# Contrast adjustment of 48 image planes: sums moved to ScalarE, a tile ahead of the stores

## The chip, the cores and the metric

One Trainium2 chip, one core. The time is device microseconds of one execution; the figure for the kernel before is the median of three runs. The profile is of one profiled execution, with times in microseconds from the start of its span.

## The reference

The input x has 16 x 3 planes of 512 x 512 float32 values in [0, 1); the factor is 1.5.

```python
mean = np.mean(x, axis=(2, 3), keepdims=True)
return np.clip(mean + factor * (x - mean), 0, 1).astype(np.float32)
```

Every output value is factor * x + (1 - factor) * mean, clipped to [0, 1], with the mean taken over its own plane. So each plane must be read whole and summed before any value of it can be written. In and out together are 100.66 MB.

## The kernel before

The data is cut into 12 tiles of 128 partitions by 8192 float32 (4.19 MB). A plane fills 32 partitions of a tile, so a tile holds four planes. A ring in SBUF, `ring`, has room for 6 tiles; tile t lies in buffer t % 6.

The program is written in the order in which each engine is to work (`manual_schedule`): the instructions of an engine stand in the order of the source, and the framework adds the semaphore waits that the accesses to the tiles need.

Loads are issued by SyncE (line 76, in `load`): tile 0 in two parts (columns 0 to 2047, then the rest), tile 1, tiles 2 and 3 in one transfer, tiles 4 and 5 in one transfer. Later, the load of tile t + 6 follows the work on tile t in the program; it waits for the store of tile t, which empties its buffer. Stores are issued from ScalarE's queue (line 101, in `store`).

The work on a tile is `compute(t)`. VectorE sums columns 0 to 4351 of each partition (line 81) into one column of `sums`; ScalarE, beside it, sums the remaining 3840 columns with an activation that copies to `junk` and accumulates (line 84). Two matmuls (lines 86 and 87) with the constant matrix `blockw`, which holds (1 - factor) / 262144 in four 32 x 32 blocks and zero elsewhere, add the two partial sums over the 32 partitions of a plane and give the shift of every partition in column t of the PSUM tile `bias`. VectorE then multiplies by the factor and adds the shift in place (line 91), and clips in place (line 94). Then the store is issued. Tile 0 is finished in two parts, of 2048 and 6144 columns, each with its own store.

```python
for t in range(n_tiles):
    compute(t)
    if t + BUFS < n_tiles:
        load(t + BUFS)
```

So before, ScalarE's queue holds: sum of tile t, store of tile t, sum of tile t + 1, store of tile t + 1. VectorE's holds: reduction of t, two passes over t, reduction of t + 1.

Of the kernel before, what the change touches and what calls it, by code (L numbers as in the profile page):

```python
# [1 line left out]

# [4 lines left out]


P = 128  # L10
ROW = 8192
BUFS = 6
SHORT = 2048
FIRST = (SHORT, ROW - SHORT)
SUM = 4352


@with_exitstack
def kernel(
    ctx: ExitStack,  # L20
    tc: tile.TileContext,
    x: bass.AP,
    factor: float,
    out: bass.AP,
):

    nc = tc.nc
    f32 = mybir.dt.float32  # L30
    Alu = mybir.AluOpType
    Act = mybir.ActivationFunctionType

    B, C, H, W = x.shape
    n_img, n_pix = B * C, H * W
    ppi = n_pix // ROW
    per_tile = P // ppi
    n_tiles = n_img // per_tile
    assert ppi * ROW == n_pix and per_tile * n_tiles == n_img

    factor = float(factor)
    wconst = (1.0 - factor) / float(n_pix)

    x_f = x.rearrange("b c h w -> (b c h w)")
    out_f = out.rearrange("b c h w -> (b c h w)")

    def dram(ap, t, c0=0, c1=ROW):
        return bass.AP(tensor=ap.tensor, offset=t * P * ROW + c0, ap=[[ROW, P], [1, c1 - c0]])

    consts = ctx.enter_context(tc.tile_pool(name="consts", bufs=1))  # L50
    xpool = ctx.enter_context(tc.tile_pool(name="xpool", bufs=1))
    small = ctx.enter_context(tc.tile_pool(name="small", bufs=1))
    psum = ctx.enter_context(tc.tile_pool(name="psum", bufs=1, space=bass.MemoryType.PSUM))


    sums = small.tile([P, 2 * n_tiles], f32, name="sums")
    junk = small.tile([P, ROW - SUM], f32, name="junk")
    bias = psum.tile([P, n_tiles], f32, name="bias")

    blockw = consts.tile([P, P], f32, name="blockw")  # L60
    nc.gpsimd.memset(blockw, 0.0)  # L61
    for a in range(0, P, ppi):
        nc.gpsimd.memset(blockw[a : a + ppi, a : a + ppi], wconst)  # L63


    ring = xpool.tile([P, BUFS, ROW], f32, name="ring")

    def load(t, c0=0, c1=ROW, n=1):

        b = t % BUFS  # L70
        src = bass.AP(
            tensor=x_f.tensor,
            offset=t * P * ROW + c0,
            ap=[[ROW, P], [P * ROW, n], [1, c1 - c0]],
        )
        nc.sync.dma_start(out=ring[:, b : b + n, c0:c1], in_=src)  # L76

    def compute(t):
        xt = ring[:, t % BUFS, :]
        own = sums[:, 2 * t : 2 * t + 2]  # L80
        nc.vector.tensor_reduce(  # L81
            out=own[:, 0:1], in_=xt[:, 0:SUM], axis=mybir.AxisListType.X, op=Alu.add
        )
        nc.scalar.activation(out=junk, in_=xt[:, SUM:ROW], func=Act.Copy, accum_out=own[:, 1:2])  # L84
        shift = bias[:, t : t + 1]
        nc.tensor.matmul(shift, blockw, own[:, 1:2], start=True, stop=False)  # L86
        nc.tensor.matmul(shift, blockw, own[:, 0:1], start=False, stop=True)  # L87
        c = 0
        for n in FIRST if t == 0 else [ROW]:
            part = xt[:, c : c + n]  # L90
            nc.vector.tensor_scalar(  # L91
                out=part, in0=part, scalar1=factor, scalar2=shift, op0=Alu.mult, op1=Alu.add
            )
            nc.vector.tensor_scalar(  # L94
                out=part, in0=part, scalar1=0.0, scalar2=1.0, op0=Alu.max, op1=Alu.min
            )
            store(t, c, c + n)
            c += n

    def store(t, c0, c1):  # L100
        nc.scalar.dma_start(out=dram(out_f, t, c0, c1), in_=ring[:, t % BUFS, c0:c1])

    with tc.manual_schedule():
        load(0, c1=SHORT)
        load(0, c0=SHORT)
        load(1)
        load(2, n=2)
        load(4, n=2)
        for t in range(n_tiles):
            compute(t)  # L110
            if t + BUFS < n_tiles:
                load(t + BUFS)


# [1 line left out]
_INS = ['x', 'factor']  # L116
_OUTS = [((16, 3, 512, 512), 'float32')]

_NUMBERS = {'factor': 1.5}


# [26 lines left out]
```

## Time and profile before

| | |
|---|---|
| time, median of 3 runs | 239.16 us (239.13 to 239.31) |
| span of the profiled execution | 237.3 us, so the median lies 1.9 us above it |
| instructions in the profile | 285 |
| TensorE (matmul) busy | 14.1 us (6%), 48 records |
| VectorE busy | 163.1 us (69%), 38 instructions |
| ScalarE busy | 43.2 us (18%), 25 instructions |
| moved | 50.33 MB read, 50.33 MB written, 424 GB/s over the span |
| first load issued | 0.74 us |
| last store issued | 218.17 us |

The profiled execution has no time of its own beside its span in the records; what lies around the span is taken as the difference to the median. In the profile, PE is TensorE, DVE is VectorE, ACT is ScalarE and SP is SyncE; a q behind the name means that the engine's queue issues a transfer. A float32 matmul shows as two records, so the 24 matmuls of the program are 48 records. A group's line gives the source line, engine, operation, output and inputs with their sizes, how many there are, the busy time and the mean length of one in ns, and then how long the engine sat idle just before them and what ended that. A table of stretches gives, for each stretch of the span, the busy time of each engine, TensorE's granted clock, the share of the DMA engines in use and GB/s.

### The profile page before, as it was taken

Reading aid. Unit: us, or ns where it says so; the run is one execution under the profiler, and the core shown is the slowest. Engines: PE = TensorE matmul, PEld = TensorE weight load, DVE = VectorE, ACT = ScalarE, POOL = GpSimd, SP = SyncE. Lnnn points to the kernel's source line nnn. Section 1 sums busy time; section 2 is a strip of 40 time slices with the busy share of each in tenths; the row PEclk is TensorE's granted clock in tenths of the full one; section 3 lists DMA queues with packets and bytes.
Section 4 is the critical chain, followed back from the end, with each engine's and each line's share of the span. In section 5 each row is a group of like instructions: output and inputs, shape, how many; then the busy total and the mean of one; then the engine's idle time right before and its main releaser. Section 6 shows DMA issues by size and latency. Waiting matters only on the chain.

```text
span 237.3 us, 285 instructions
## 1 busy us (share of the span) xinstructions
PE 14.1 (6%) x48; PEld 12.0 (5%) x48; DVE 163.1 (69%) x38; ACT 43.2 (18%) x25; POOL 0.9 (0%) x9
## 2 busy tenths in 40 slices
PE   0010010001010001010010100100100100010000
PEld 0010010001010001010010100100100100010000
DVE  0079989048989328999989898891892795687000
ACT  2050230041050023050320504101400500500000
POOL 1000000000000000000000000000000000000000
DMA  7999999999999999999999999999999999999996
GB/s 297 410 442 442 421 442 359 456 439 441 442 436 414 403 431 442 442 442 442 436 442 436 414 409 425 442 442 442 442 436 442 436 420 403 425 442 442 442 442 265
DMA packets 3712, 100.66 MB, mean 424 GB/s; under 512 B 384, under 2 KB 384, under 8 KB 384
## 3 DMA queue, kind: packets, MB, share of 16 engines
q1 hardware_dynamic: 1840, 50.33, 49.7%
q10 hardware_dynamic: 1872, 50.33, 49.2%
HBM read 50.33 MB, written 50.33 MB: 424 GB/s over the span
## 4 chain that ended last, share of the span: by engine, by line
DMA 57%; DVE 29%; another core or an unknown queue 3%; PE 1%; SPq 1%; issue 0%; DVEq 0%
DMA ring<-in_x_dram 41%; DMA out_dram<-ring 16%; DVE sums L81 10%; DVE ring L91 9%; DVE ring L94 9%; PE bias L87 1%; SPq L76 1%; DVEq L91 0%
## 5 line engine op out<-in xcount | busy, mean ns | idle before, releaser
L81 DVE TENSOR_REDUCE sums<-ring 128x1 f32<-128x4352 f32 x12 | 56.2, 4683 | 45.7 <-DMA ring<-in_x_dram 45.7
L84 ACT ACTIVATE junk<-ring 128x3840 f32<-128x3840 f32 x12 | 40.8, 3403 | 163.3 <-DMA ring<-in_x_dram 107.5
L91 DVE TENSOR_SCALAR ring<-ring,bias 128x8192 f32<-128x8192 f32 (+2 forms) x13 | 54.1, 4163 | 8.9 <-PE bias L87 7.4
L94 DVE TENSOR_SCALAR ring<-ring 128x8192 f32<-128x8192 f32 (+2 forms) x13 | 53.3, 4099 | 0.4
L86 PE MATMUL bias<-sums,blockw 128*128 128x1 f32 x24 | 7.0, 361 | 190.8 <-ACT junk L84 190.8
L86 PEld LDWEIGHTS bias<-sums,blockw 128*128 128x128 f32 x24 | 6.0, 312 | 191.7 <-ACT junk L84 175.2
L87 PE MATMUL bias<-sums,blockw 128*128 128x1 f32 x24 | 7.0, 363 | 4.3 <-DVE sums L81 3.9
L87 PEld LDWEIGHTS bias<-sums,blockw 128*128 128x128 f32 x24 | 6.0, 311 | 5.3 <-DVE sums L81 5.0
L84 ACT ACTIVATION_READ_ACCUMULATOR junk<-ring 128x1 f32 x12 | 2.2, 186 | 0.0
L84 ACT ACT_TABLE_LOAD x1 | 1.3, 1283 | 0.7 <-PEq L129 0.7
L63 POOL MEMSET blockw<- 32x32 f32 x4 | 0.5, 117 | 0.2
L61 POOL MEMSET blockw<- 128x128 f32 x1 | 0.2, 204 | 0.3 <-POOLq L129 0.3
L129 POOL MEMSET const-bfloat16-1.0<- 128x1 bf16 x1 | 0.1, 111 | 0.0
L129 POOL MEMSET const-uint8-127<- 128x1 uint8 x1 | 0.1, 111 | 0.0
L129 POOL MEMSET const-float32-1.0<- 128x1 f32 x1 | 0.1, 108 | 0.0
L129 POOL MEMSET const-float32-0.0<- 128x1 f32 x1 | 0.1, 103 | 0.2 <-issue 0.2
## 6 DMA issues: line engine op xcount, KB each, us to landing
out_dram<-ring ACTq DMA_DIRECT2D x11, 4096.0 KB, 35.8
ring<-in_x_dram SPq DMA_DIRECT2D x7, 4096.0 KB, 49.7
ring<-in_x_dram SPq DMA_DIRECT2D x2, 8192.0 KB, 66.7
ring<-in_x_dram SPq DMA_DIRECT2D x1, 3072.0 KB, 11.7
out_dram<-ring ACTq DMA_DIRECT2D x1, 3072.0 KB, 28.2
ring<-in_x_dram SPq DMA_DIRECT2D x1, 1024.0 KB, 4.8
out_dram<-ring ACTq DMA_DIRECT2D x1, 1024.0 KB, 17.5
```

The lines of the kernel that those rows point to most:

```text
L61: nc.gpsimd.memset(blockw, 0.0)
L63: nc.gpsimd.memset(blockw[a : a + ppi, a : a + ppi], wconst)
L76: nc.sync.dma_start(out=ring[:, b : b + n, c0:c1], in_=src)
L81: nc.vector.tensor_reduce(out=own[:, 0:1], in_=xt[:, 0:SUM], axis=mybir.AxisListType.X, op=Alu.add)
L84: nc.scalar.activation(out=junk, in_=xt[:, SUM:ROW], func=Act.Copy, accum_out=own[:, 1:2])
L86: nc.tensor.matmul(shift, blockw, own[:, 1:2], start=True, stop=False)
L87: nc.tensor.matmul(shift, blockw, own[:, 0:1], start=False, stop=True)
L91: nc.vector.tensor_scalar(out=part, in0=part, scalar1=factor, scalar2=shift, op0=Alu.mult, op1=Alu.add)
L94: nc.vector.tensor_scalar(out=part, in0=part, scalar1=0.0, scalar2=1.0, op0=Alu.max, op1=Alu.min)
L129: nc = _bacc.Bacc("TRN2", target_bir_lowering=False, num_devices=1)
```

## The change

`compute` is taken apart into `add`, `shift_by`, `clip` and `store`. Tile 0 keeps the shared sum: VectorE reduces columns 0 to 4351 and ScalarE the rest, and two matmuls make its shift. From tile 1 on, ScalarE sums the whole tile (8192 columns) with one activation, which now copies each value onto itself in the ring instead of into `junk`; VectorE does no reduction; and one matmul makes the shift. `junk` and `FIRST` are gone.

The order changes too. In the program, the sum and the matmul of tile t + 1 now stand ahead of the clip and the store of tile t. For tile 0, the first part (2048 columns) is clipped and stored first, then tile 1 is summed, then the second part of tile 0 is clipped and stored. ScalarE's queue thus holds: sum of t + 1, store of t, sum of t + 2, store of t + 1. The loads and their order are the same, as are the sizes of the transfers.

```diff
-    def compute(t):
-        xt = ring[:, t % BUFS, :]
-        own = sums[:, 2 * t : 2 * t + 2]
-        nc.vector.tensor_reduce(
-            out=own[:, 0:1], in_=xt[:, 0:SUM], axis=mybir.AxisListType.X, op=Alu.add
+    def clip(t, c0, c1):
+        part = ring[:, t % BUFS, c0:c1]
+        nc.vector.tensor_scalar(
+            out=part, in0=part, scalar1=factor, scalar2=bias[:, t : t + 1],
+            op0=Alu.mult, op1=Alu.add,
         )
-        nc.scalar.activation(out=junk, in_=xt[:, SUM:ROW], func=Act.Copy, accum_out=own[:, 1:2])
-        shift = bias[:, t : t + 1]
-        nc.tensor.matmul(shift, blockw, own[:, 1:2], start=True, stop=False)
-        nc.tensor.matmul(shift, blockw, own[:, 0:1], start=False, stop=True)
...
+        nc.vector.tensor_scalar(
+            out=part, in0=part, scalar1=0.0, scalar2=1.0, op0=Alu.max, op1=Alu.min
+        )
+
+    def add(t, c0=0):
+        part = ring[:, t % BUFS, c0:ROW]
+        own = sums[:, 2 * t : 2 * t + 1]
+        nc.scalar.activation(out=part, in_=part, func=Act.Copy, accum_out=own)
+        return own
+
+    def shift_by(t, *parts):
+        for k, part in enumerate(parts):
+            nc.tensor.matmul(
+                bias[:, t : t + 1], blockw, part, start=k == 0, stop=k == len(parts) - 1
             )
...
-        for t in range(n_tiles):
-            compute(t)
+
+        rest = sums[:, 1:2]
+        nc.vector.tensor_reduce(
+            out=rest, in_=ring[:, 0, 0:SUM], axis=mybir.AxisListType.X, op=Alu.add
+        )
+        shift_by(0, add(0, SUM), rest)
+        clip(0, 0, SHORT)
+        store(0, 0, SHORT)
+        shift_by(1, add(1))
+        clip(0, SHORT, ROW)
+        store(0, SHORT, ROW)
+        load(BUFS)
+        for t in range(1, n_tiles):
+            if t + 1 < n_tiles:
+                shift_by(t + 1, add(t + 1))
+            clip(t, 0, ROW)
+            store(t, 0, ROW)
             if t + BUFS < n_tiles:
                 load(t + BUFS)
```

More of the change, by code (lines that the diff above doesn't have):

```diff
@@ L13 @@
 SHORT = 2048
-FIRST = (SHORT, ROW - SHORT)
 SUM = 4352
@@ L56 @@
     sums = small.tile([P, 2 * n_tiles], f32, name="sums")
-    junk = small.tile([P, ROW - SUM], f32, name="junk")
     bias = psum.tile([P, n_tiles], f32, name="bias")
@@ L76, in load @@
         nc.sync.dma_start(out=ring[:, b : b + n, c0:c1], in_=src)
-    def compute(t):
-        xt = ring[:, t % BUFS, :]
-        own = sums[:, 2 * t : 2 * t + 2]
-        nc.vector.tensor_reduce(
-            out=own[:, 0:1], in_=xt[:, 0:SUM], axis=mybir.AxisListType.X, op=Alu.add
-        )
-        nc.scalar.activation(out=junk, in_=xt[:, SUM:ROW], func=Act.Copy, accum_out=own[:, 1:2])
-        shift = bias[:, t : t + 1]
[L86 to L92, printed above, removed]
-            )
[L94 to L98, printed above, removed]
+    def clip(t, c0, c1):
[3 more added lines that the diff above has]
+            op0=Alu.mult, op1=Alu.add,
+        )
+        nc.vector.tensor_scalar(
[10 more added lines that the diff above has]
+                bias[:, t : t + 1], blockw, part, start=k == 0, stop=k == len(parts) - 1
+            )
     def store(t, c0, c1):
```

## The prediction

> **What bounds the kernel now.** I read the slices of the page first, then the table of stretches, then the groups of instructions, then the timeline around one tile and around the last one.
>
> ```profile
> DVE  0079989048989328999989898891892795687000
> ACT  2050230041050023050320504101400500500000
> DMA  7999999999999999999999999999999999999996
> ```
>
> ```profile
> 38.50:50.70 12.20, 0.00 (x0) 0.00 (x0) 3.43 (x2) 0.00 (x0) 0.00 (x0) 1.00 0.96 408
> 50.70:145.70 95.00, 7.04 (x24) 6.01 (x24) 81.27 (x19) 20.98 (x12) 0.00 (x0) 1.00 1.00 433
> 145.70:203.70 58.00, 3.52 (x12) 3.00 (x12) 40.78 (x9) 10.49 (x6) 0.00 (x0) 1.00 1.00 434
> 203.70:218.20 14.50, 1.18 (x4) 1.01 (x4) 13.60 (x3) 3.50 (x2) 0.00 (x0) 1.00 1.01 434
> ```
>
> The last two columns of a stretch are the share of the 16 DMA engines in use and GB/s. The DMA engines never rest: share 1.00 at 433 GB/s from 50.7 us to the end, at least 0.96 from 6 us on. The 100.66 MB of the page take 232.5 us at 433 GB/s, of a span of 237.3 us. So the kernel is bound by the transfers, and VectorE's 163 us lie beside them. Two things follow. No edit to the engines can gain much: what is left is some 4.8 us of start and finish, which the change does not touch. And the change is free only as long as the engines still bring the stores early enough to leave no DMA engine idle. How much room there is, the end of the timeline shows.
>
> ```profile
> 203.76 4.69 DVE L81 TENSOR_REDUCE sums<-ring 128x1 f32<-128x4352 f32 x1 [4.98 <-DMA ring<-in_x_dram]
> 213.71 4.43 DVE L94 TENSOR_SCALAR ring<-ring 128x8192 f32<-128x8192 f32 x1
> 218.17 0.34 ACTq L101 DMA_DIRECT2D out_dram<-ring  x1
> ```
>
> The last store is issued at 218.2 us and the span ends 19.1 us later; one tile of 4.19 MB alone is 9.7 us at 433 GB/s. So a whole store is still ahead of it in the queue. Counting two stores (19.4 us) and about 0.9 us for landing back from 237.3, store 9 leaves the DMA engines at about 217: store 10, issued at 198.8, is 18 us early, store 11 some 8 us.
>
> **The costs of a tile.** The groups, each shape apart, and one tile's timeline give every duration.
>
> ```profile
> L91 DVE TENSOR_SCALAR ring<-ring,bias 128x8192 f32<-128x8192 f32 x11 | 49.4, 4491 | 8.2 <-PE bias L87 6.7 <-issue 1.5
> L94 DVE TENSOR_SCALAR ring<-ring 128x8192 f32<-128x8192 f32 x11 | 48.7, 4427 | 0.4
> L84 ACT ACTIVATE junk<-ring 128x3840 f32<-128x3840 f32 x12 | 40.8, 3403 | 163.3 <-DMA ring<-in_x_dram 107.5 <-DVE ring L94 55.8
> L84 ACT ACTIVATION_READ_ACCUMULATOR junk<-ring 128x1 f32 x12 | 2.2, 186 | 0.0
> ```
>
> ```profile
> 50.73 3.40 ACT L84 ACTIVATE junk<-ring 128x3840 f32<-128x3840 f32 x1 [19.16 <-DMA ring<-in_x_dram]
> 54.28 0.58 PE L86 MATMUL bias<-sums,blockw 128*128 128x1 f32 x2 [21.44 <-ACT junk L84]
> 55.42 0.59 PE L87 MATMUL bias<-sums,blockw 128*128 128x1 f32 x2 [0.55 <-DVE sums L81]
> 56.11 4.49 DVE L91 TENSOR_SCALAR ring<-ring,bias 128x8192 f32<-128x8192 f32 x1 [0.75 <-PE bias L87]
> 60.64 4.43 DVE L94 TENSOR_SCALAR ring<-ring 128x8192 f32<-128x8192 f32 x1
> 65.10 0.34 ACTq L101 DMA_DIRECT2D out_dram<-ring  x1
> 65.48 3.40 ACT L84 ACTIVATE junk<-ring 128x3840 f32<-128x3840 f32 x1 [11.25 <-DVE ring L94]
> ```
>
> Read off: matmul 0.15 us after the sum's 3.40 us have passed (50.73 to 54.28); clip 0.69 us after the matmul starts (55.42 to 56.11); store issued 8.99 us after the clip starts (56.11 to 65.10); ScalarE's next instruction 0.38 us after that.
>
> **Removed.** Eleven VectorE reductions of 4.68 us (51.5 us) and eleven of the twenty-four matmuls. VectorE is not the bound, so this alone is worth nothing; it only shortens a tile's way from landing to store.
>
> **Added: the longer sum.** ScalarE sums 8192 elements where it summed 3840. No row has that length. If the whole 3403 ns scales, it is 7.26 us; if twice the accumulator's 186 ns is fixed, (3403-372) x 2.133 + 372 = 6.84 us. I take one such fixed part, (3403-186) x 2.133 + 186 = 7.05 us, the nearest to what ScalarE itself shows as a price without elements. Writing in place into the ring instead of into junk I cost at nothing: the same 128 partitions of f32 are written per element; 0.1 us either way would be inside these ends. The Trainium skill ("ScalarE: Activation LUTs", What ACT_TABLE_LOAD costs) gives 186 ns + 0.833 ns per element, 3.39 us for the row's 3.40, hence 7.01 us; the sum below would be 0.4 us less by it. The same page (Rules for kernel authors) speaks against the change: plain adds belong on VectorE.
>
> **Moved: the order, and two new waits.** This decides. On ScalarE the order is now add(t+1), store(t), add(t+2). ScalarE works its queue in order, so add(t+2), though its tile may have landed long ago, stands behind store(t), which waits for clip(t) on VectorE. That is the first wait. The second is not in the source: the built program's waits show that the first clip instruction of tile t waits for the matmul of tile t+1, not only for its own; the plainest sign is that the clip of the last tile waits for no TensorE semaphore at all, because the one before it has already waited for that matmul. All shifts are columns of the one tile `bias`, and the matmul of t+1 stands ahead of clip(t) in the program. So clip(t) stands behind add(t+1), and store(t) behind clip(t), and add(t+2) behind store(t): a closed ring through three engines with no overlap at all between ScalarE's sum and VectorE's clip. "A tile ahead" buys nothing; one turn is
>
> 7.05 (add) + 0.15 + 0.69 (matmul) + 8.99 (clip) + 0.38 (issue) = 17.26 us per tile.
>
> The DMA engines need 19.4 us per tile (8.39 MB in and out at 433 GB/s). So each turn is faster than the transfers, and once data is there the ring does not wait for loads. But it starts late and cannot catch up fast enough: before, tile 0 and 1 were stored while the first six loads still ran; now each store needs the next tile's landing.
>
> **When it starts.** Tile 0's loads, sum and first store (issued at 20.9) are unchanged. Tile 1 has landed about 9.6 us after tile 0 (12.9), at 22.5; add(1) runs from there, and the rest of tile 0's clip waits for its matmul: 22.5 + 7.05 + 0.84 = 30.4, its two clip instructions take 6.8 us (20.79 to 27.63 before), so store 0's second part is issued at 37.2 instead of 27.6. Add(2) needs tiles 2 and 3, which one load brings; before, they landed at 50.7. The stretch 38.5 to 50.7 moved 4.98 MB, shared by this load and store 0's second part; by their rows (32 and 24 KB, taken in turns, an estimate) 57% or 2.84 MB were the load's. Store 0's first part took 17.5 us to land (page, DMA issues) for an exchange that is 12.1 us by this sharing (5.24 MB at 433 GB/s), so a store joining busy queues starts some 4 us late: at 41.2. Until then the load has the DMA to itself (2.7 us, 1.17 MB), the other 1.67 MB at 57% take 6.9 us: add(2) starts at 48.2. The ends are 50.7 (no relief) and 45.1 (all 2.84 MB alone).
>
> **The sum.** Add(11) starts nine turns later: 48.2 + 9 x 17.26 = 203.5. Clip(10) starts at 203.5 + 7.05 + 0.84 = 211.4, store 10 is issued at 220.4, clip(11) follows at once and store 11 goes at 229.4, against 198.8 and 218.2 before. The DMA engines are done with everything else at about 217 (above), so they stand idle for 3 to 5 us until store 10 gets going, which was 18 us early before. Two stores from an idle start: the first as tile 0's load did, 12.1 us from issue to use (0.74 to 12.88), the second 9.7 us more: 220.4 + 21.8 = 242.2, and some 0.4 us to the end of the span: 242.6. Around the span lie 1.9 us (239.16, the median, less 237.3): 244.5 us, 2.2% slower. Loads do not bind: store 5, which frees the buffer of tile 11, is issued at about 134 and tile 11 is needed at 203.5, 69 us for a store and a load that take 39 us at half the rate each. Smaller edits (one matmul each, junk gone, SP's order) cost nothing beside this; SP's loads wait on later stores, but SP has nothing else queued.
>
> **Rivals.**
> A, no slower. The transfers stay the bound: the stores, though late, keep the queue filled to the end, and the time is 239.2 plus or minus 0.5. It decides where store 10 is issued before about 216, 4.6 us earlier than I have it: with ten sums of 6.6 us, with add(2) at 43.6, or if clip(t) did not truly wait for the next tile's matmul, which would let VectorE clip under the next load. For: 17.26 is below 19.4. Against: 6.6 is below my low end of 6.84, and the waits stand in the program. Chance 0.09; 0.08 same, with a 0.01 tail to faster.
> B, worse still: the sum is 7.26 us (2.1 us more over ten sums) and the first stores bring no relief to load 2 (2.5 us): 246.6 to 249, chance 0.12. The stretch 38.5 to 50.7 speaks for it, with only 408 GB/s where the stores had just begun.
> C, the change gains: the stretches below 433 GB/s between 20.9 and 50.7 (420 and 408) come from mixing stores in, and fewer stores there save up to 0.9 us without a later idle time: 238.3. Needs A first; chance 0.02.
>
> **How the numbers follow.** My case has 0.77, at 244.5. Its ends: 6.84 us gives -2.1, 7.26 gives +2.1, add(2) between 45.1 and 50.7 gives -3.1 to +2.5, the four small gaps of a turn at 0.05 us each 0.5 to 1 us; not all on one side. The range 241.0 to 247.5 takes these, and leaves out A, C and the far part of B. A measurement of this kernel can tell about 0.2% (0.5 us). Faster 0.03, same 0.08, slower 0.89.
>
> **What would show it.** After: ScalarE's ACTIVATE on 128x8192 near 7.05 us; VectorE's clip idle before it "<-PE bias" some 8 us at each of ten tiles, adding to over 80 us; starts of successive sums 17.3 us apart from about 48 us on, with tiles landed long before; the last store issued near 229; a slice with DMA below 9 around 217 to 222. Wrong if the clip of tile t runs while the sum of t+1 does, if sums are spaced by 19.4 us waiting for loads, or if the DMA slices stay full to the end.

## The result and the profile after

The changed kernel takes 242.85 us (median of four runs, 242.81 to 244.06) against 239.14 us before: ratio 1.0163, 95% interval [1.0146, 1.018], slower by 1.6%. The profiled execution took 242.83 us with a span of 241.0 us.

The slices of the page after, VectorE, ScalarE and the DMA engines:

```profile
DVE  0074091007709509429239159068076095099800
ACT  2052900091290380560650830920902903800000
DMA  7999999989999999999999999999999999986996
```

VectorE has lost its reductions but that of tile 0 and is busy for 112 us instead of 163, with holes wherever ScalarE is busy: the two take turns. What ends the kernel is in the third row. The DMA slices, full to the end before, open in the last fifth. The table of stretches (us; busy time and count by engine; TensorE's clock, DMA share, GB/s in the last columns) sizes the hole:

```profile
145.70:203.70 58.00, 1.76 (x6) 1.50 (x6) 31.53 (x8) 22.47 (x7) 0.00 (x0) 1.00 1.00 434
203.70:220.00 16.30, 0.59 (x2) 0.50 (x2) 9.57 (x3) 6.02 (x2) 0.00 (x0) 1.00 0.75 322
```

A quarter of 16.3 us is 4.1 us of idle DMA engines; the span is 3.7 us longer. The groups of instructions and the list of waits give the cause:

```profile
L89 ACT ACTIVATE ring<-ring 128x8192 f32<-128x8192 f32 x11 | 77.3, 7029 | 115.1 <-DVE ring L82 90.7 <-DMA ring<-in_x_dram 24.4
L78 DVE TENSOR_SCALAR ring<-ring,bias 128x8192 f32<-128x8192 f32 x11 | 49.4, 4491 | 92.8 <-PE bias L94 92.8
```

```profile
DVE ring L78 <- PE bias L94: 103.0, 12, 18.5
ACT ring L89 <- DVE ring L82: 90.7, 9, 10.1
```

VectorE's clip waits for a matmul at every tile but the last, and ScalarE's sum waits for VectorE's clip (through the store that stands ahead of it) at nine tiles: 10.1 us each time, the length of a clip with its handovers. ScalarE's three waits for loads all end by 48 us. One turn and the end, from the timeline:

```profile
47.78 7.03 ACT L89 ACTIVATE ring<-ring 128x8192 f32<-128x8192 f32 x1 [18.21 <-DMA ring<-in_x_dram]
...
64.95 7.03 ACT L89 ACTIVATE ring<-ring 128x8192 f32<-128x8192 f32 x1 [10.04 <-DVE ring L82]
...
72.12 0.58 PE L94 MATMUL bias<-sums,blockw 128*128 128x1 f32 x2 [16.58 <-ACT ring L89]
72.75 4.49 DVE L78 TENSOR_SCALAR ring<-ring,bias 128x8192 f32<-128x8192 f32 x1 [8.21 <-PE bias L94]
77.27 4.43 DVE L82 TENSOR_SCALAR ring<-ring 128x8192 f32<-128x8192 f32 x1
81.73 0.34 ACTq L99 DMA_DIRECT2D out_dram<-ring  x1
82.11 7.03 ACT L89 ACTIVATE ring<-ring 128x8192 f32<-128x8192 f32 x1 [10.04 <-DVE ring L82]
...
202.60 7.03 ACT L89 ACTIVATE ring<-ring 128x8192 f32<-128x8192 f32 x1 [10.10 <-DVE ring L82]
...
219.38 9.20 ACTq L99 DMA_DIRECT2D out_dram<-ring  x2
```

Sum, matmul, clip, store issue, next sum: no two overlap. At 72.75 VectorE starts on tile 2, and the matmul it waited for, at 72.12, is that of tile 3. Nine turns lead from 47.78 to 202.60, 17.20 us each. The stores of tiles 10 and 11 (merged in the last line) go at 219.4 and 228.2; before, 198.8 and 218.2. In shorter stretches no DMA packet starts between 215.5 and 220.2 us: the queue is dry, that is, nothing issued is left to move, until store 10 gets going.

### The profile page after: what moved, and what is told of

Same layout as the page of the kernel before. It is cut to its first block, busy times and chain, and to the rows that moved or that the text cites. A ratio compares the mean times of both kernels' runs of the same rounds, so it can differ in the third digit from the quotient of the medians.

```text
span 241.0 us, 218 instructions
## 1 busy us (share of the span) xinstructions
PE 7.6 (3%) x26; PEld 6.5 (3%) x26; DVE 112.0 (46%) x27; ACT 83.1 (34%) x25; POOL 0.9 (0%) x9
## 3 DMA queue, kind: packets, MB, share of 16 engines
q1 hardware_dynamic: 1840, 50.33, 48.9%
## 4 chain that ended last, share of the span: by engine, by line
DVE 39%; ACT 27%; DMA 19%; issue 5%; PE 2%; ACTq 1%; SPq 1%
ACT ring L89 27%; DVE ring L78 21%; DMA ring<-in_x_dram 19%; DVE ring L82 18%; PE bias L94 2%; ACTq L99 1%; SPq L74 1%; ACTq L89 0%
## 5 line engine op out<-in xcount | busy, mean ns | idle before, releaser
L89 ACT ACTIVATE ring<-ring 128x8192 f32<-128x8192 f32 (+1 forms) x12 | 80.7, 6727 | 125.9 <-DVE ring L82 90.7
L94 PE MATMUL bias<-sums,blockw 128*128 128x1 f32 x26 | 7.6, 361 | 202.8 <-ACT ring L89 202.1
L94 PEld LDWEIGHTS bias<-sums,blockw 128*128 128x128 f32 x26 | 6.5, 311 | 203.8 <-ACT ring L89 186.7
L109 DVE TENSOR_REDUCE sums<-ring 128x1 f32<-128x4352 f32 x1 | 4.7, 4686 | 12.8 <-DMA ring<-in_x_dram 12.8
L89 ACT ACTIVATION_READ_ACCUMULATOR ring<-ring 128x1 f32 x12 | 2.2, 186 | 0.0
## 6 DMA issues: line engine op xcount, KB each, us to landing
out_dram<-ring ACTq DMA_DIRECT2D x1, 1024.0 KB, 17.5
```

Source lines behind the costliest of these rows:

```text
L89: nc.scalar.activation(out=part, in_=part, func=Act.Copy, accum_out=own)
L94: nc.tensor.matmul(bias[:, t : t + 1], blockw, part, start=k == 0, stop=k == len(parts) - 1)
L109: nc.vector.tensor_reduce(out=rest, in_=ring[:, 0, 0:SUM], axis=mybir.AxisListType.X, op=Alu.add)
```

## The experiments

The theory has three parts: the closed ring (the clip of t waits for the matmul of t + 1; the sum of t + 2 stands behind the store of t), its length, and its late start. Twelve kernels ran, in three groups; the kernel before ran beside each group, at 239.23, 239.32 and 239.25 us.

| | time, us | ratio to before, 95% interval | store 10 issued, us |
|---|---|---|---|
| changed kernel | 242.85 | 1.0163 [1.0146, 1.018] | 219.4 |
| two bias tiles | 239.10 | 0.9992 [0.9983, 1.0002] | 204.0 |
| clip ahead of matmul | 239.04 | 0.9991 [0.9982, 1.0] | 203.7 |
| whole sum, own turn | 239.14 | 0.9994 [0.9984, 1.0003] | 207.4 |
| shared sum, ahead | 239.17 | 0.9998 [0.9989, 1.0008] | 207.0 |
| longer sum | 253.08 | 1.0586 [1.056, 1.0611] | 228.9 |
| sum of 7936 | 242.35 | 1.0121 [1.01, 1.0141] | 219.1 |
| sum of 7424 | 238.87 | 0.9982 [0.9973, 0.9992] | 214.4 |
| tiles 2, 3 apart | 244.63 | 1.0224 [1.0209, 1.0239] | 221.2 |
| tiles 2 to 5 apart | 241.67 | 1.0114 [1.009, 1.0137] | 219.6 |
| last turn opened | 238.95 | 0.9988 [0.998, 0.9997] | 212.1 |
| before, tile 0 whole | 240.01 | 1.003 [1.0017, 1.0042] | |
| clip first, tile 0 whole | 239.76 | 1.0014 [1.0005, 1.0023] | |

The time is a median; the issue of store 10 is read from the one profiled run of each kernel. In the five kernels that the closed ring made slower, the time of the profiled run lies 23.4 to 23.6 us after that issue (242.83 less 219.38 in the changed kernel, 252.37 less 228.93 with the longer sum, 244.74 less 221.19 with tiles 2 and 3 apart), whatever made store 10 late.

**Two bias tiles.** The first two kernels of the list after the changed one open the ring in two ways; the third takes the next tile's sum out from ahead of the store, and the fourth shortens the turn.

```diff
-    bias = psum.tile([P, n_tiles], f32, name="bias")
+    biases = [psum.tile([P, 512], f32, name=f"bias{k}") for k in range(2)]
+
+    def bias_of(t):
+        return biases[t % 2][:, t : t + 1]
...
-            out=part, in0=part, scalar1=factor, scalar2=bias[:, t : t + 1],
+            out=part, in0=part, scalar1=factor, scalar2=bias_of(t),
...
-                bias[:, t : t + 1], blockw, part, start=k == 0, stop=k == len(parts) - 1
+                bias_of(t), blockw, part, start=k == 0, stop=k == len(parts) - 1
```

> The changed kernel with the shifts of even and odd tiles in two PSUM tiles, so that the clip of a tile waits for its own matmul alone. Theory (the closed ring of sum, clip and store, which starts late, makes store 10 late): the clip of t runs while tile t + 1 is still loading, the ring is open, store 10 is issued before 216 and the time is back at 239.2 (238.7 to 239.7); VectorE's idle time before the clip for the matmul falls from 103 us by more than half. Rival (stores are late because ScalarE's queue holds store t behind the sum of t + 1, or because the whole sum stands on ScalarE): both are unchanged here, so 242 to 243.

239.10 us, as the theory has it, with ScalarE's order and its whole sums unchanged, which ends the rival. The waits of this kernel, of the two that answer to those shown above:

```profile
ACT ring L92 <- DMA ring<-in_x_dram: 127.4, 10, 22.8
DVE ring L81 <- PE bias L97: 95.7, 10, 19.4
```

ScalarE now waits for loads at ten tiles, no longer for VectorE: the transfers pace it. One part of my expectation was wrong: VectorE's idle time ahead of the clip stays at 95.7 us, and it did not fall by half, because it is now the wait for the tile's own landing and sum. The size of a wait does not tell whether it is in a ring; who ended the wait before it does.

**Clip ahead of the matmul.**

```diff
-        shift_by(1, add(1))
+        own = add(1)
         clip(0, SHORT, ROW)
+        shift_by(1, own)
...
-                shift_by(t + 1, add(t + 1))
+                own = add(t + 1)
             clip(t, 0, ROW)
+            if t + 1 < n_tiles:
+                shift_by(t + 1, own)
```

> The changed kernel with the matmul of tile t + 1 placed behind the clip of tile t in the program, the order on ScalarE and VectorE as in the changed kernel and one PSUM tile for the shifts. Theory: the clip no longer waits for the next tile's matmul, which opens the ring as two PSUM tiles do: 239.2 (238.7 to 239.7). Rival (the PSUM tile itself, or ScalarE's order, makes the loss): 242 to 243. If two PSUM tiles help and this does not, it is the place of the shifts and not the wait.

239.04 us with one PSUM tile. It is the wait and not the place of the shifts.

**Whole sum, own turn.**

```diff
-        shift_by(1, add(1))
...
-            if t + 1 < n_tiles:
-                shift_by(t + 1, add(t + 1))
+            shift_by(t, add(t))
             clip(t, 0, ROW)
             store(t, 0, ROW)
```

> The whole sum on ScalarE in place and one matmul, but in the order of the kernel before: sum, clip and store of a tile in its own turn. Theory: the turn is still 17.2 us without overlap, but a store no longer waits for the landing of the next tile, and 17.2 is less than the 19.4 us of the transfers: store 11 about 2.4 us later than before (220.6), no idle DMA, 239.2 (238.7 to 239.7). Rival (the turn of 17.2 us is itself the loss, whatever the order): 241 or more.

239.14 us. From this kernel's timeline:

```profile
190.56 7.03 ACT L89 ACTIVATE ring<-ring 128x8192 f32<-128x8192 f32 x1 [10.10 <-DVE ring L82]
207.35 0.34 ACTq L99 DMA_DIRECT2D out_dram<-ring  x1
207.79 7.03 ACT L89 ACTIVATE ring<-ring 128x8192 f32<-128x8192 f32 x1 [10.10 <-DVE ring L82]
224.57 0.34 ACTq L99 DMA_DIRECT2D out_dram<-ring  x1
```

The turn is the same 17.2 us, with the same waits of ScalarE for VectorE; but a sum is followed by the store of its own tile, so store 10 goes at 207.4 instead of 219.4. Store 11 is later than I expected (224.6 against 220.6), later too than before (218.2), and the time is the same: it still finds store 10 under way. So neither the whole sums nor the turn make the loss by themselves; store 10 beyond the point where the queue runs dry does.

**Shared sum, ahead.**

```diff
+    def shared(t):
+        rest = sums[:, 2 * t + 1 : 2 * t + 2]
+        nc.vector.tensor_reduce(
+            out=rest, in_=ring[:, t % BUFS, 0:SUM], axis=mybir.AxisListType.X, op=Alu.add
+        )
+        return add(t, SUM), rest
...
-        shift_by(1, add(1))
+        shift_by(1, *shared(1))
...
-                shift_by(t + 1, add(t + 1))
+                shift_by(t + 1, *shared(t + 1))
```

> The new order alone: the sum of t + 1 ahead of the clip of t, but shared between VectorE (4352) and ScalarE (3840) with two matmuls, as before. The clip still waits for the next tile's matmuls. Theory: the ring turns in 4.7 + 0.7 + 9.0 = 14.4 us, 2.8 us less than with the whole sum on ScalarE, so after ten turns store 10 is some 28 us earlier or waits for loads: 239.2 (238.7 to 239.9). Rival (waiting for the next tile is the loss by itself, whatever the length of the sum): 241 or more.

239.17 us. The order alone, with the ring closed, costs nothing while the turn is short (the store issues at 63.90 and 78.20 in its timeline are 14.3 us apart). The change needs both its parts to lose.

**A longer and two shorter sums.**

```diff
+MORE = 1024
...
+        if t:
+            nc.scalar.activation(out=junk, in_=part[:, 0:MORE], func=Act.Copy)
         nc.scalar.activation(out=part, in_=part, func=Act.Copy, accum_out=own)
```

The two shorter sums differ in one constant, 7936 or 7424:

```diff
+FEWER = 7936
...
-        part = ring[:, t % BUFS, c0:ROW]
+        part = ring[:, t % BUFS, c0 : ROW if t == 0 else FEWER]
```

> The changed kernel with a second activation of 1024 elements per tile on ScalarE ahead of each whole sum (its copy is not used). Theory: ten sums lie one behind the other in the ring between the landing of tiles 2 and 3 and the issue of store 10; the rows of 3840 and 8192 elements give 0.833 ns per element, so each turn grows by about 1.0 us and the time by ten times that: 252.8 (252 to 254), and the start of the second sum moves by 1 us at most. Rival (a fixed price, such as waiting for the first landings, with the sums beside the transfers): under 245.

> The changed kernel with ScalarE summing 7936 of the 8192 columns from tile 1 on (256 columns are left out of the mean). Theory: 0.21 us less in each of ten turns, 2.1 us less in all, still above the floor of the transfers: 240.7 (240.3 to 241.2). Rival (the loss is not proportional to the length of the sum): 242 to 243.

> The changed kernel with ScalarE summing 7424 of the 8192 columns from tile 1 on (768 columns are left out of the mean). Theory: ten turns of 0.64 us less would give 236.4, which is below the floor of the transfers; store 10 is issued near 213, before the queue runs dry, so 239.2 (238.8 to 239.7), no lower. Rival (no floor, the chain alone makes the time): 236 to 237.

253.08 us for the longer sum, against 252.8 expected: 1.06 us for each of the 1024-element activations, and 10.2 us in all between the medians. The four runs are two near 252.4 and two near 253.7; in the profiled one (252.37) store 10 goes 9.55 us later than in the changed kernel, ten activations less a second sum that starts 1.05 us earlier, at 46.73. The sum of 7424 meets the floor at 238.87 us, not the 236.4 us of a chain without one; store 10 goes at 214.4. The sum of 7936 is a miss: 242.35 us (241.39 to 242.53) for 240.7, within the band of the rival (242 to 243), by which the loss does not follow the length of the sum. The time alone would speak for the rival, so the timeline has to decide. ScalarE's:

```profile
49.07 6.82 ACT L90 ACTIVATE ring<-ring 128x7936 f32<-128x7936 f32 x1 [19.72 <-DMA ring<-in_x_dram]
...
202.46 6.82 ACT L90 ACTIVATE ring<-ring 128x7936 f32<-128x7936 f32 x1 [10.16 <-DVE ring L83]
...
219.09 9.20 ACTq L100 DMA_DIRECT2D out_dram<-ring  x2
```

Its turn is 153.39 / 9 = 17.04 us, shorter by 0.16 us of the 0.21 that the sum lost; but the ring started at 49.07 instead of 47.78, 1.3 us later. From the start to store 10 it is 170.02 us against 171.60: the gain per turn is there, and the later landing of tiles 2 and 3 took most of it away in this run of 242.53 us. That the run of 241.39 us had the earlier start is likely and not shown. Only the length per turn is shown here; the time of 240.7 was not reached.

**The start of the ring.**

```diff
-        load(2, n=2)
+        load(2)
+        load(3)
         load(4, n=2)
```

> The changed kernel with tiles 2 and 3 loaded by two transfers instead of one; the ring is untouched. Theory: tile 2 lands about 10 us earlier, the ring starts near 38 instead of 47.8, and store 10 is issued before 216 (209 to 213, where the loads of tiles 4 and 5 hold it up): 239.2 (238.8 to 239.9). Rival (the turn alone decides, and the start is made good later by waiting for loads): 241 or more.

244.63 us, slower than the changed kernel. My theory of the start fell here. ScalarE's timeline:

```profile
37.73 7.03 ACT L89 ACTIVATE ring<-ring 128x8192 f32<-128x8192 f32 x1 [7.97 <-DVE ring L82]
...
54.91 7.03 ACT L89 ACTIVATE ring<-ring 128x8192 f32<-128x8192 f32 x1 [10.05 <-DVE ring L82]
...
83.94 7.03 ACT L89 ACTIVATE ring<-ring 128x8192 f32<-128x8192 f32 x1 [21.90 <-DMA ring<-in_x_dram]
```

The ring starts ten microseconds earlier, as wanted, and then stands for 21.9 us: the load of tiles 4 and 5 takes 80.5 us from issue to landing, where the longest load of the changed kernel, that of the same two tiles, takes 72.6 us. Stores 1 and 2 now go at 54.5 and 71.7 instead of 64.6 and 81.7, and share the DMA engines with it. So I loaded all of them apart:

```diff
-        load(2, n=2)
-        load(4, n=2)
+        for t in range(2, BUFS):
+            load(t)
```

> The changed kernel with tiles 2 to 5 loaded one by one. With tiles 2 and 3 alone apart, the second sum started at 37.7 as wanted, but the fourth waited until 83.9 for the load of tiles 4 and 5, which now shared the DMA engines with earlier stores. Theory as it stands now (the ring costs at its end too: store 10 stands behind the landing of tile 11 by 7.0 + 0.8 + 9.0 = 16.8 us; an earlier start lets stores and loads share evenly, so tile 11 lands near 203 instead of 190, and store 10 goes near 220 all the same): no wait of ScalarE as long as 5 us for a landing before tile 6, then sums spaced by 19.4 us, and 242 (241 to 244). Rival (the start alone, held up by the transfers of two tiles): store 10 near 210 and 239.2 (238.7 to 239.7).

241.67 us, in the theory's band. The profiled run is the longest of the four, 243.23 us; the others took 241.47 to 241.75. In it no sum waits for a pair, and from tile 7 on the sums are spaced by the transfers:

```profile
183.48 7.03 ACT L89 ACTIVATE ring<-ring 128x8192 f32<-128x8192 f32 x1 [12.24 <-DMA ring<-in_x_dram]
200.27 0.34 ACTq L99 DMA_DIRECT2D out_dram<-ring  x1
202.85 7.03 ACT L89 ACTIVATE ring<-ring 128x8192 f32<-128x8192 f32 x1 [12.25 <-DMA ring<-in_x_dram]
219.63 9.20 ACTq L99 DMA_DIRECT2D out_dram<-ring  x2
```

Store 10 goes at 219.6, within 0.3 us of the changed kernel, for another reason: it stands behind the sum of tile 11, which lands at 202.8, 16.8 us earlier. An early start gives the stores their part of the DMA engines, and the last load then comes as late as it does before the change (203.8). A late start lets the loads run ahead, and then the chain of turns is late. Either way the closed ring holds store 10 back: to 219.4 and 219.6 in the profiled runs, and to an estimated 218 in the three shorter runs with all loads apart (their times less 23.5 us), whose landings no profile shows.

**The last turn opened.**

```diff
             if t + 1 < n_tiles:
-                shift_by(t + 1, add(t + 1))
+                own = add(t + 1)
+            if t + 2 < n_tiles:
+                shift_by(t + 1, own)
             clip(t, 0, ROW)
+            if t + 2 == n_tiles:
+                shift_by(t + 1, own)
```

> The changed kernel with the ring opened in its last turn alone: the matmul of tile 11 stands behind the clip of tile 10, all else as changed. Theory: up to store 9 (202.2) nothing moves, the clip of tile 10 then runs beside the sum of tile 11, store 10 goes at about 211.1 and store 11 at about 220, before the queue runs dry: 239.2 (238.7 to 239.7). Rival (the loss is spread over all turns, one turn gives one eleventh back): 242 or more.

238.95 us: one matmul moved behind one clip returns all of the loss. Its timeline at the end:

```profile
203.16 4.48 DVE L78 TENSOR_SCALAR ring<-ring,bias 128x8192 f32<-128x8192 f32 x1
203.27 0.34 ACTq L99 DMA_DIRECT2D out_dram<-ring  x1
203.71 7.03 ACT L89 ACTIVATE ring<-ring 128x8192 f32<-128x8192 f32 x1 [10.10 <-DVE ring L82]
...
212.13 9.20 ACTq L99 DMA_DIRECT2D out_dram<-ring  x2
```

The nine turns up to it are as closed as in the changed kernel (the sum at 203.71 still waited 10.10 us for VectorE); only the clip of tile 10, at 203.16, runs beside the sum of tile 11. Store 10 goes 7.3 us earlier than in the changed kernel, before the queue is dry.

**Tile 0 whole.** Two kernels asked whether the floor itself can be lowered.

```diff
-FIRST = (SHORT, ROW - SHORT)
+FIRST = (ROW,)
...
-        load(0, c1=SHORT)
-        load(0, c0=SHORT)
+        load(0)
```

The second kernel has the same load in the kernel with the clip ahead of the matmul, and one clip and one store for tile 0, ahead of the sum of tile 1.

> The kernel before with tile 0 loaded and stored whole instead of in two parts. The DMA engines are full from 2 us to the end either way, and the stretches 20.9 to 50.7, where the small transfers run beside the loads, moved 420 and 408 GB/s where 433 is the rule, 1.2 us in all. Theory: the end is set by the transfers, the order of the stores at the start does not matter; if the small parts cause the slower stretches, up to 1.2 us come back: 238.6 (238.0 to 239.3). Rival (the first store needs to be early): 240 or more.

> The opened ring (matmul of t + 1 behind the clip of t) with tile 0 loaded and stored whole as well; VectorE sums part of tile 0 only. Theory as for the kernel before with tile 0 whole: 238.6 (238.0 to 239.3), the transfers' floor. Rival (the later first store, behind the sum of tile 1 or the landing of tile 2, leaves too little to store at the end): 240 or more.

240.01 and 239.76 us: not the 238.6 expected but slower by 0.3% and 0.1%, and the first of them reaches the rival's 240. So a whole tile 0 lowers nothing. The two profiled runs (239.39 and 239.13 us, spans of 237.4 us, full of DMA to the last slice) are among the shortest of twelve each. In the first of them, 38.5 to 50.7 moves 443 GB/s instead of 408, as hoped, but 20.9 to 38.5 stays slow at 415, the first 6 us fall from 298 to 262, and the span gains nothing. The other runs go up to 240.71 and 239.99 us, with recorded spans up to 238.7 and 238.2: the excess of the medians lies in the span of runs that were not profiled, and what makes it, the rival's late first store or another cause, is open.

## Why the prediction was right, and where it was not

The mechanism is the one predicted, and the sum went through the events that it named. Its terms against the trace:

| term | predicted | measured |
|---|---|---|
| sum of 8192 elements | 7.05 | 7.03 |
| end of sum to clip | 0.15 + 0.69 | 0.14 + 0.63 |
| clip to store issue | 8.99 | 8.98 |
| issue to next sum | 0.38 | 0.38 to 0.46 |
| turn | 17.26 | 17.20 |
| add(2) starts | 48.2 | 47.78 |
| store 10 issued | 220.4 | 219.38 |
| store 10 to the end of the span | 22.2 | 21.6 |
| span | 242.6 | 241.0 |

The time was 1.65 us too high: 0.4 from the start, 0.6 from the turns, 0.6 from the last two stores, which took 21.6 us from the issue of store 10 to the end of the span where 22.2 was counted. The matmul's 0.69 was read from a tile of before where VectorE had just ended its reduction; where VectorE is idle it is 0.63 (72.12 to 72.75), which tile 0 of before also shows (17.70 to 18.33). None of the gaps is large; ten of them count.

Three readings of the working were loose, and none carried the result. The DMA engines are not full to the very end before the change: the stretch from 218.2 us has a share of 0.89 and 384 GB/s. The late start of a store was put at some 4 us, where 17.5 less 12.1 is 5.4; with 5.4 the second sum would start at 46.9. And kernels whose instructions are the same up to there start it at 47.78 and at 48.89, so that 48.2 came within 0.4 us is in part luck.

The sum's length was the term with the widest ends, and it fell on the middle. The Trainium skill ("ScalarE: Activation LUTs", What ACT_TABLE_LOAD costs) gives 186 ns and 0.833 ns per element. The four lengths of these runs are 1.06, 6.39, 6.82 and 7.03 us for 1024, 7424, 7936 and 8192 elements; the page makes 1.04, 6.37, 6.80 and 7.01 of them. It holds here to 0.02 us, in place as well as into another tile.

The ring was read from the built program's waits. Two kernels that remove just that wait return the whole loss, and so does a third that removes it in one turn alone; so it is shown, not argued. The point from which it decides was set at store 10 before about 216 us: store 10 at 214.4 costs nothing, at 219.1 it does; no profiled run lies between. The last packets ahead of store 10 start before 215.5 us in the changed kernel, which fits.

One step failed. The rival of no loss had three conditions, and one of them, the second sum at 43.6 us, is not enough: at 37.7 us the kernel was slower still, and with all loads apart, at 37.6 us, it lost 1.1%. I moved the start of the chain and left the landings where they were. But stores that go earlier take DMA time from the loads: the load of tiles 4 and 5 took 72.6 us to land with late stores and 80.5 with earlier ones, and 84.8 in the kernel before, whose stores go earliest (20.9, 27.6 and 41.9 us). The Trainium skill ("DMA: Bandwidth & Descriptors", Queues, rings and completion order) has each DMA engine go round its queues packet by packet; these three times agree with that. The other two conditions held: sums of 6.39 us, below the 6.6 asked, gave 238.87, and opening the wait 239.04 and 239.10. The prediction also told the loss as built up over ten turns. That is how it comes about in this kernel, but it can be undone in one: what counts in these runs is when store 10 is issued.

No version that does all the work beats the kernel before clearly: the opened rings are at 0.9988 to 0.9992 of it, about 0.1%, which is near the transfers' floor.

## What to carry to other kernels

When transfers fill the time, ask when the last two stores are issued, and when the queue ahead of them runs dry; in these runs nearly all else was free, until it moved one of these. Issuing the next tile's sum ahead buys overlap only if nothing of the present tile waits for it: look in the built program for a wait on the next tile's result, which a shared tile can add without a line of source. A start that is moved earlier moves the landings too.

## What the runs showed of the hardware

The landing of the pair of tiles 2 and 3, which one load brings, goes with the time at which the second part of tile 0 is stored beside it: with that store at 34.7 us (shared sum, ahead) the second sum starts at 49.4, at 37.2 (changed kernel) at 47.8, and at 38.3 (longer sum) at 46.7. That a later store leaves the load the DMA engines for longer, as the prediction had it, agrees with this; three kernels do not show it alone, given the step below.

It also varies without a cause that the program shows: with the store at 37.1 (last turn opened, the same instructions up to there) the second sum starts at 48.9. The step of 1.1 us is near the time of one row of 32 KB on one of 16 DMA engines (32768 B at 433 / 16 GB/s is 1.21 us, an estimate); that it is one row is not shown. One of the changed kernel's four runs took 244.06 us, 1.2 us over the other three, and the longer sum's four runs lie in two pairs 1.2 us apart; the longer ones were not profiled, so that it is the same step is likely and not shown. A late start passes unchanged through a closed ring (49.07 us with the sum of 7936, store 10 at 219.1), and is without effect where the transfers set the end (48.89 us with the last turn opened, 239.03 us in that run).
